# A pool of their own at the top of SBUF for the transposed activations of a two-layer decoder trunk

## The chip, the cores and the metric

The kernel runs on one core of a Trainium2 chip. The metric is the device time of one execution, in microseconds. The kernel before takes 958.66 us (median of three runs, 957.46 to 959.23). The engines are TensorE (PE, with its weight loads as PEld), VectorE (DVE), ScalarE (ACT), GpSimd (POOL) and SyncE (SP), which issues most DMAs.

## What is computed

The reference is a decoder trunk of two layers on 256 tokens of 1024 features, in float32. Layer 0 mixes tokens by differential attention and chunked gated linear attention, layer 1 by a chunked gated DeltaNet. After each mixer come a cross-attention into 256 memory tokens and a gated feed-forward part with a causal convolution of width 3, each followed by a layer norm over `alpha * x + sublayer(x)`.

```python
def memory_cross_attention(x, mem, wq, wkv, wo):
    q = (x @ wq).reshape(B_, S_, N_XA, D_XA)
    k, v = _split(mem @ wkv, (D_MODEL, D_MODEL))
    ...
    return o @ wo

def conv_ffn(x, w_in, conv_w, conv_b, w_out):
    h = causal_dwconv(x @ w_in, conv_w, conv_b)
    g, u = _split(h, (D_FF, D_FF))
    return (jax.nn.silu(g) * u) @ w_out
```

Nearly all of the arithmetic is in such products of 256 tokens with a weight matrix: `D_MODEL` is 1024, `D_FF` is 2816, and a feed-forward input projection has 5632 columns.

## The kernel before

Each float32 product is made of three matmuls on operands split into a high and a low part (`hi` and `lo`, type float32r): high times high, high times low, low times high. A weight piece of 128 x 1024 numbers is loaded by SP into `raw` (pool `rawp`, three buffers of 1 MB), ACT casts it to `wh` (L149) and DVE subtracts to get `wl` (L151); `whp` and `wlp` hold four pieces each. The activations stand transposed in SBUF, features on partitions, as a `Parts` object: four tiles of 128 x 4 x 256, two high and two low, 4096 bytes per partition each. `hT` is the normed input of a sublayer, `uT`, `oT` and `xoT` are the outputs of the mixers and of the cross-attention, `aT` is the feed-forward part's middle (its first four tiles in the same pool, the other eight in a pool of the stage).

There are two forms of projection:

- `mm3` (L156 to L158) has the weights stationary: a 128 x 128 piece of `wh` or `wl` is loaded into the array, and 256 columns of `hT` (or of the transposed memory, `memT`) stream past it. One feature tile of 128 columns takes 8 x 3 = 24 matmuls, and 512 columns take 96. `proj_t_gen` and the loop in `ffn` use it: the results are `ps_t` and `ps_f`.
- `mm3n` (L162 to L164) and `proj_lead` (L298) have the activations stationary, 128 x 128 of them, and 512 columns of `wh` or `wl` stream. `proj_n_gen` (`ps_n`) and `out_proj` (`ps_o`) use it.

The cross-attention takes the same two forms for its scores (`xs`: keys `k` stream past the queries `xq`; in layer 1 the split keys bear the name `wh` too) and its values (`xo`: `pT` streams past `v`).

The feed-forward part calls `proj_first` (512 columns by L298, then transposed, L315), then `proj_t` for 512 more, and then runs 36 feature tiles of 24 matmuls, two weight loads for four tiles. ACT and DVE convolve and gate each result (L1306 to L1317). Elsewhere a chain (a mixer or a cross-attention) is written as a generator, and `weave` puts steps of projections between its steps; TensorE's order is then the order of the code. Each engine works through its own instructions in order, and a semaphore wait holds all that stands behind it.

All pools but the temporary ones are stacked from the bottom of SBUF: constants, `rawp`, `whp`, `wlp`, `tp`, `hp`, `lnp`. The stages' own pools (`pool(...)`, side right) are stacked downwards from the top. `tp` is the pool that the change is about: eight buffers under one tag, handed out in turn to `hT`, `uT`, `xoT`, `oT`, four tiles of `aT`, and three tiles that the DeltaNet holds (`keep`). `new_t` (L383) takes four of them.

Of the kernel before, what the change touches and what calls it, by code (L numbers as in the profile page):

```python
# [74 lines left out]
class Parts:  # L75
    """hi and lo parts of [128, k, 256], four k to a tile"""
# [12 lines left out]
def hybrid_trunk(ctx: ExitStack, tc: tile.TileContext, a: dict, const: dict, out: bass.AP, dbg=None):  # L89
# [6 lines left out]
    tp = ctx.enter_context(tc.tile_pool(name="tp", bufs=8))  # L96
# [5 lines left out]
    def pool(name, bufs=2, side="right"):  # L102
        return tc.tile_pool(name=name, bufs=bufs, side=side, reuse_waits="tile")

# [30 lines left out]
    # ------------------------------------------------------------ weights  # L135
# [6 lines left out]
    normed = []  # last instructions of the layer norms  # L142
# [11 lines left out]
    def mm3(ps, lh, ll, rh, rl, first, last):  # L154
        """weights stationary"""
        nc.tensor.matmul(ps, lh, rh, start=first, stop=False)  # L156
        nc.tensor.matmul(ps, lh, rl, start=False, stop=False)  # L157
        nc.tensor.matmul(ps, ll, rh, start=False, stop=last)  # L158

    def mm3n(ps, lh, ll, rh, rl, first, last):  # L160
        """activations stationary"""
        nc.tensor.matmul(ps, lh, rh, start=first, stop=False)  # L162
        nc.tensor.matmul(ps, lh, rl, start=False, stop=False)  # L163
        nc.tensor.matmul(ps, ll, rh, start=False, stop=last)  # L164
# [5 lines left out]
    def ahead(gen, n):  # L170
        """gen with its items made n steps before they are given"""
        items = []
        for item in gen:
            items.append(item)
            if len(items) > n:
                yield items.pop(0)
        yield from items

    def proj_t_gen(xs, w, c0, n, cb, step=256):
        """cb(m, ps): ps[feature, token] of the columns c0 + 128 m."""  # L180
        def pieces():
            for q in range(0, n, step):
                nq = min(step, n - q)
                raw = load(w, c0 + q, nq)
                for m in range(0, nq, P):
                    nm = min(P, nq - m)
                    yield (q + m) // P, nm, split(raw[:, :, m:m + nm])

        for m, nm, (wh, wl) in ahead(pieces(), AHEAD):
            ps = acc("ps_t")[:nm, :T]  # L190
            for k in range(KT):
                mm3(ps, wh[:, k], wl[:, k], xs.h(k), xs.l(k), k == 0, k == KT - 1)
                if k % 2 and k < KT - 1:
                    yield
            cb(m, ps)
            yield
# [4 lines left out]
    def proj_16(xs, w, c0):  # L201
        """[32, token]: two parts, their sum being the product with 16 columns"""
        raw = load(w, c0, 16)
        hl = whp.tile([P, 1024], F32R, tag="wh", name="w16")[:, :KT * 32].rearrange("p (k i n) -> p k i n", k=KT, i=2)
        nc.scalar.copy(hl[:, :, 0], raw)
        nc.vector.tensor_tensor(hl[:, :, 1], raw, hl[:, :, 0].bitcast(F32), op=ALU.subtract)
        ps = acc("ps_16")[:32, :T]
        for k in range(KT):
            for i, x in enumerate((xs.h(k), xs.l(k))):
                nc.tensor.matmul(ps, hl[:, k].rearrange("p i n -> p (i n)"), x, start=k == i == 0,  # L210
                                 stop=k == KT - 1 and i == 1)
        return ps

    def proj_n_gen(xs, w, c0, n, cb):
        """cb(q, tt, ps): ps[token, feature] of the columns c0 + 512 q."""
# [27 lines left out]
    class Fill:  # L243
        """generators to take steps of, one after the other"""
# [15 lines left out]
    def weave(chain, fill):  # L260
        """the tensor engine's work of the chain, each step of it (n) followed by n steps of fill"""
        with tc.manual_schedule(engines={mybir.EngineType.PE}):
            due = 0.0
            for n in chain:
                due += n
                while due >= 1.0:
                    fill.step()
                    due -= 1.0

    def steps(n, *gens):  # L270
        """the steps of gens in turn"""
        gens = list(gens)
        while gens:
            for gen in list(gens):
                m = next(gen, gens)
                if m is gens:
                    gens.remove(gen)
                else:
                    yield n if m is None else m

    def proj_lead(xs, w, c0, n, cb, step=4, after=()):
        """as proj_n for up to 512 columns, token tile 0 first; after: calls to make after the loads, by number"""
# [19 lines left out]
    def proj_first_gen(xs, w, c0, n, cb):  # L302
        """as proj_t for up to 512 columns, by way of [token, feature], token tile 0 first"""
# [18 lines left out]
    def out_proj(xs, w, nk, order, ntail=NTAIL):  # L322
        """[head, tail]: generators, tail(cb, pools) with generators cb(tt, [half 0, half 1]); the tail has the last 4 of nk"""
# [43 lines left out]
    # ------------------------------------------------- activations, layer norm  # L367
    def to_t_gen(dst, src, tt):
        """token-major src [128, 1024] to the columns of token tile tt of dst"""
# [13 lines left out]
    def new_t(name):  # L383
        return Parts(*[[tp.tile([P, 4, T], F32R, tag="T", name=name) for _ in range(2)] for _ in range(2)])
# [48 lines left out]
    # ------------------------------------------------------------ start  # L433
    # convolution weights, features on partitions
# [31 lines left out]
    def mem_kv0(memT, kp, vp):  # L466
        """hi and lo parts of k [features, memory] and v [memory, features]"""
# [5 lines left out]
    def mem_kv1(memT, kp):  # L473
        """as they are: k0, k1, v0, v1"""
# [14 lines left out]
    def lower(x, lev):  # L489
        """the columns in the lower halves of the blocks of 2 << lev"""  # L490
        return x.rearrange("... (n u j) -> ... n u j", u=2, j=1 << lev)[..., 0, :]

    def upper(x, lev):
        """the columns in the upper halves of the blocks of 2 << lev"""
        return x.rearrange("... (n u j) -> ... n u j", u=2, j=1 << lev)[..., 1, :]

    # ------------------------------------------------------------ layer 0 mixer
    lam_col, conv_w = [], []

    def mixer_ab(h, hT, ap_, fill, res):  # L500
# [7 lines left out]
        # gains of the head norms, features on partitions  # L508
# [4 lines left out]
        def head_out(po, tt, gate, gi, factor, sm):  # L513
            """po [128 t, 4 heads, 128]: rms norm per head, gain (and gate), transposed into uT"""
# [26 lines left out]
        # ---- A projections (token-major, rotary on 16 of 64)  # L541
# [13 lines left out]
        with pool("gla") as sm:  # L555
            # ---- GLA projections
            # rows: the two parts of the low-rank gates' product, the bias
# [58 lines left out]
            def rotary():  # L616
                # rotary tables [128, tt, 8]
# [27 lines left out]
                # lambda on every partition  # L645
# [11 lines left out]
            # ---- GLA  # L657
# [22 lines left out]
            def intra(u):  # L680
                tt, pr = u
                tsl = slice(tt * P, tt * P + P)
                # level l has entries in the columns t of the upper halves of the blocks of 2 << l only
# [49 lines left out]
            def gla():  # L733
                """steps of the tensor engine's work; a step's results are not used in the next one"""
# [43 lines left out]
    def diff_attention(uT, qkv, head_out, sm, nlam):  # L778
        """steps of the tensor engine's work; a step's results are not used in the next one"""
# [82 lines left out]
    # ------------------------------------------------------------ layer 1 mixer  # L862
    def mixer_c(h, hT, sm, smq, fill, res):
# [9 lines left out]
        # per token and head: beta, g and its sums  # L873
# [10 lines left out]
        table = []          # the last to use the table of exp or of silu: the other's users wait  # L884
# [70 lines left out]
        # of group 0, where the next group's are made meanwhile  # L955
# [12 lines left out]
        def col(x):  # L968
            """[P, 4] as [P, 4, 128]"""
            return x.unsqueeze(2).broadcast_to([x.shape[0], 4, P])  # L970
# [25 lines left out]
        def gdn_pre(grp, tt, o):  # L996
# [4 lines left out]
            # decay [s, t] = exp(gc_t - gc_s), t >= s in the chunk  # L1001
# [26 lines left out]
            # with k_n = r k, r^-2 = sum(k^2) + eps: (I + diag(r) G diag(r b)) = diag(r) (I + G diag(r^2 b)) diag(1 / r)  # L1028
            # for G = k k^T decay, so k, v / r and r^2 b take the place of k_n, v and b
            # q_n = q rq, rq = d^-1/2 rsqrt(sum(q^2) + eps); eps / rq^2 is for the norm of the output  # L1030
# [22 lines left out]
            # L[t, s] = k_t.k_s decay b_s below the diagonal; Z^T = (I + L)^-1, by doubling of its diagonal blocks  # L1053
# [4 lines left out]
            # at level l the columns (2 b + u) (1 << l) + r of Z are stored at 64 u + (64 >> l) r + b  # L1058
# [8 lines left out]
        def gdn_inv(o):  # L1067
            Z, L = o["Z"], o["L"]
            for lev in range(1, NLEV + 1):
                # the lower halves' rows and columns packed to 64; at the last level they are the first 64  # L1070
# [41 lines left out]
        def gdn_rec(grp, os_, outs):  # L1112
# [3 lines left out]
            def values(o, pvn):  # L1116
                # diag(b) (I + M diag(b))^-1 = (I + diag(b) M)^-1 diag(b)
# [4 lines left out]
            def norm(tt, pon):  # L1122
# [4 lines left out]
                # (pon * rq) * rsqrt(mean((pon * rq)^2) + eps) = pon * rsqrt(mean(pon^2) + eps / rq^2)  # L1127
# [78 lines left out]
    # ------------------------------------------------------------ cross-attention  # L1206
    def cross(h, hT, kv, l, sm, oT, fill, kvp=None):
        """the first steps, then steps of the tensor engine's work"""
# [87 lines left out]
    # ------------------------------------------------------------ feed-forward  # L1296
# [148 lines left out]
```

## Time and profile before

| what | value |
|---|---|
| median of three runs | 958.66 us |
| profiled execution: span from the first to the last instruction | 956.4 us |
| PE, PEld busy | 936.4 us, 837.1 us |
| DVE, ACT, POOL busy | 690.2 us, 530.0 us, 36.3 us |
| mean DMA traffic | 160 GB/s |

The profile's own execution has a span of 956.4 us; 2.3 us of the median lie outside of it. PE's busy time has to be read with care: a matmul row gives a duration of 283 ns for 256 columns, but the next matmul starts long before that is over, since they are pipelined. What a matmul costs TensorE is read from the timeline instead: the distance from its start to the next one's. A timeline row gives the start in us from the span's start, the duration in us, the engine, the line, the operation with its output and inputs, and how many equal instructions were merged.

### The profile page before, as it was taken

The numbers are of one execution on the slowest core, as the hardware profiler recorded it, in microseconds if no ns is written. First come the engines' busy times: TensorE is split into PE (matmuls) and PEld (weight loads), VectorE is DVE, ScalarE is ACT, GpSimd is POOL, SyncE is SP. The second block draws the span as 40 slices with busy tenths as digits, with TensorE's granted clock in tenths as the row PEclk, the third lists the DMA queues.
The fourth block names the chain that finished last, engine by engine and source line by source line (L and its number), as shares of the span: only waits on it lengthen the run. The fifth ranks groups of instructions, "written<-read, shape, count | busy, mean of one in ns | idle before, by whom it ended". The sixth has DMA issues, their size and how long they took to land. (4 is left out here: it accounts for less than half of the span.)

```text
span 956.4 us, 15842 instructions
## 1 busy us (share of the span) xinstructions
PE 936.4 (98%) x6284; PEld 837.1 (88%) x6284; DVE 690.2 (72%) x1155; ACT 530.0 (55%) x945; POOL 36.3 (4%) x49
## 2 busy tenths in 40 slices
PE   7999999999999999999999999999999999999996
PEld 5877798899888999998889998888789799999885
DVE  5497586776468988884687875654696888888564
ACT  4753476345435766663357875664464386666440
POOL 1000001000000000000010000000200100000000
PEclk9999999999999999999999999998999999999999
DMA  8843336554664555555566441211543546555551
GB/s 252 287 136 124 97 132 201 179 167 159 220 220 130 170 189 191 191 190 176 179 192 181 133 133 45 89 45 45 176 139 127 175 162 214 190 184 178 179 173 45
DMA packets 101715, 152.89 MB, mean 160 GB/s; under 512 B 5225, under 2 KB 73673, under 8 KB 101641
## 3 DMA queue, kind: packets, MB, share of 16 engines
q1 hardware_dynamic: 99576, 145.08, 46.3%
q0 software_dynamic: 2064, 6.80, 2.2%
q8 instruction: 50, 0.82, 0.4%
q14 instruction: 25, 0.20, 0.1%
HBM read 150.81 MB, written 1.05 MB: 159 GB/s over the span
## 5 line engine op out<-in xcount | busy, mean ns | idle before, releaser
L151 DVE TENSOR_TENSOR wl<-raw,wh 128x1024 fp32r<-128x1024 f32 x268 | 325.5, 1223 | 120.7 <-ACT wh L149 119.4
L149 ACT CAST wh<-raw 128x1024 fp32r<-128x1024 f32 x268 | 278.8, 1052 | 239.0 <-PE ps_f L157 71.5
L156 PE MATMUL ps_f<-hT,wh 128*128 128x256 f32 x576 | 163.0, 283 | 0.0
L157 PE MATMUL ps_f<-hT,wh 128*128 128x256 f32 x576 | 163.0, 283 | 0.0
L158 PE MATMUL ps_f<-hT,wl 128*128 128x256 f32 x576 | 163.0, 283 | 0.0
L156 PEld LDWEIGHTS ps_f<-hT,wh 128*128 128x128 f32 x576 | 110.6, 192 | 0.0
L157 PEld LDWEIGHTS ps_f<-hT,wh 128*128 128x128 f32 x576 | 110.6, 192 | 0.0
L158 PEld LDWEIGHTS ps_f<-hT,wl 128*128 128x128 f32 x576 | 110.6, 192 | 0.0
L156 PE MATMUL ps_t<-hT,wh 128*128 128x256 f32 x352 | 103.5, 294 | 0.0
L157 PE MATMUL ps_t<-hT,wh 128*128 128x256 f32 x352 | 99.5, 283 | 0.0
L158 PE MATMUL ps_t<-hT,wl 128*128 128x256 f32 x352 | 99.4, 283 | 0.0
L162 PE MATMUL ps_o<-wh,aT 128*128 128x512 f32 x176 | 69.1, 393 | 0.0
L163 PE MATMUL ps_o<-wl,aT 128*128 128x512 f32 x176 | 68.9, 391 | 0.0
L164 PE MATMUL ps_o<-wh,aT 128*128 128x512 f32 x176 | 68.6, 390 | 0.0
L156 PEld LDWEIGHTS ps_t<-hT,wh 128*128 128x128 f32 x352 | 67.2, 191 | 1.1
L157 PEld LDWEIGHTS ps_t<-hT,wh 128*128 128x128 f32 x352 | 67.3, 191 | 0.1
L158 PEld LDWEIGHTS ps_t<-hT,wl 128*128 128x128 f32 x352 | 67.2, 191 | 0.0
L298 PE MATMUL ps<-wh,hT 128*128 128x512 f32 x192 | 54.8, 404 | 0.0
L298 PEld LDWEIGHTS ps<-wh,hT 128*128 128x128 f32 x192 | 36.4, 193 | 8.3 <-DVE hT L377 0.5
L1306 ACT ACTIVATE fy<-ps_f,fcw 128x256 f32<-128x256 f32 x72 | 40.4, 561 | 0.0
L162 PEld LDWEIGHTS ps_o<-wh,aT 128*128 128x128 f32 x176 | 33.0, 188 | 7.6 <-issue 0.5
L924 DVE SCALAR_TENSOR_TENSOR cv<-ps_t,gcw,cv 128x253 f32<-128x253 f32 (+2 forms) x72 | 33.4, 475 | 8.6 <-ACT cv L921 8.1
(359 smaller groups left out, 1847.7 us busy)
## 6 DMA issues: line engine op xcount, KB each, us to landing
raw<-in_ffn_w_in SPq DMA_DIRECT2D x44, 1024.0 KB, 5.2
raw<-in_w_in SPq DMA_DIRECT2D x26, 1024.0 KB, 5.7
raw<-in_ffn_w_out SPq DMA_DIRECT2D x22, 1024.0 KB, 5.0
raw<-in_xa_wkv SPq DMA_DIRECT2D x16, 1024.0 KB, 5.3
raw<-in_w_mix_out SPq DMA_DIRECT2D x8, 1024.0 KB, 5.1
raw<-in_xa_wq SPq DMA_DIRECT2D x8, 1024.0 KB, 7.1
raw<-in_xa_wo SPq DMA_DIRECT2D x8, 1024.0 KB, 5.3
lngb<-in_ln_g POOLq DMA_DIRECT2D x6, 512.0 KB, 4.8
```

What stands on the lines that cost most here:

```text
L149: nc.scalar.copy(hi, src)
L151: nc.vector.tensor_tensor(lo, src, hi.bitcast(F32), op=ALU.subtract)
L156: nc.tensor.matmul(ps, lh, rh, start=first, stop=False)
L157: nc.tensor.matmul(ps, lh, rl, start=False, stop=False)
L158: nc.tensor.matmul(ps, ll, rh, start=False, stop=last)
L162: nc.tensor.matmul(ps, lh, rh, start=first, stop=False)
L163: nc.tensor.matmul(ps, lh, rl, start=False, stop=False)
L164: nc.tensor.matmul(ps, ll, rh, start=False, stop=last)
L298: nc.tensor.matmul(ps, x, ww[:, k], start=k0 + k == 0 and ww is wh and not xl, stop=k0 + k == KT - 1 and ww is wl)
L924: nc.vector.scalar_tensor_tensor(y[:, d:], ps[:, :T - d], cw[:, j, m:m + 1], y[:, d:], op0=ALU.mult, op1=ALU.add)
L1306: nc.scalar.activation(yt, ps, AF.Identity, scale=cw[:, 2, mc:mc + 1], bias=cw[:, 3, mc:mc + 1])
```

## The change

`tp` has four buffers and not eight. A new pool `xp` of four buffers is opened right after the function `pool`, on the right side and before any stage's pool, so that it lies at the very top of SBUF. `new_t` takes the four tiles of `hT` from `xp`, and those of every other name from `tp`. The diff also strips comments and docstrings, which leaves the lines in place.

```diff
-    tp = ctx.enter_context(tc.tile_pool(name="tp", bufs=8))
+    tp = ctx.enter_context(tc.tile_pool(name="tp", bufs=4))
...
     def pool(name, bufs=2, side="right"):
         return tc.tile_pool(name=name, bufs=bufs, side=side, reuse_waits="tile")
 
+    xp = ctx.enter_context(pool("xp", 4))
+
...
     def new_t(name):
-        return Parts(*[[tp.tile([P, 4, T], F32R, tag="T", name=name) for _ in range(2)] for _ in range(2)])
+        p = xp if name == "hT" else tp
+        return Parts(*[[p.tile([P, 4, T], F32R, tag="T", name=name) for _ in range(2)] for _ in range(2)])
```

The built programs of before and after have the same 9072 instructions in the same order on every engine, and each waits for the same semaphores at the same values. What differs is where the tiles lie. The layout, in bytes from the start of a partition, with the remainder of the address modulo 128, of the tiles that TensorE reads:

| tile | before | mod 128 | after | mod 128 |
|---|---|---|---|---|
| `wh`, `wl` (weight pieces) | 43552 to 76319 | 32 | the same | 32 |
| `hT` | in turn in 76320 to 109087 | 32 | 212960 to 229343 | 96 |
| `uT`, `oT`, `xoT`, first four of `aT` | in turn in 76320 to 109087 | 32 | in turn in 76320 to 92703 | 32 |
| other eight of `aT` | from 188384 | 96 | from 172000 | 96 |
| `memT` | from 162528 | 96 | from 146144 | 96 |
| `k` and `v` of layer 0's cross-attention | from 129760, 146144 | 96 | from 113376, 129760 | 96 |
| `xq` (queries) | from 194464 | 32 | from 178080 | 32 |
| `wh` of `xs` (keys of layer 1) | from 161696 | 32 | from 145312 | 32 |
| `pT` (probabilities) | from 217056 | 96 | from 200672 | 96 |

Inside a tile the pieces that one matmul reads start at multiples of 128 bytes, so the remainder holds for all of them. All pools that stand above `tp`, on both sides, move down by 16384 bytes, which changes no remainder.

## Rows read from the trace of the kernel before

**Rows 1.** The head of the page.

```profile
span 956.4 us, 15842 instructions
```

**Rows 2.** Waits of PE, whole span: total us, times, longest us.

```profile
PE pt L373 <- DMA c_all<-in_const_all: 4.7, 1, 4.7
PE pt L373 <- DMA h<-in_x: 2.4, 1, 2.4
```

**Rows 3.** Instructions that read or write `hT`: durations ns, first and last start.

```profile
L156 PE MATMUL ps_f<-hT,wh x576: 283/283/283, 319.9 to 887.8; 128*128 128x256 f32 x192
...
L156 PE MATMUL ps_t<-hT,wh x352: 277/283/388, 23.3 to 784.1; 128*128 128x256 f32 x176
...
L298 PE MATMUL ps<-wh,hT x192: 387/389/775, 10.7 to 771.2; 128*128 128x512 f32 x192
L298 PE MATMUL ps<-wl,hT x96: 387/389/628, 13.4 to 771.6; 128*128 128x512 f32 x96
L162 PE MATMUL ps_n<-wh,hT x80: 387/397/502, 36.6 to 650.5; 128*128 128x512 f32 x80
```

**Rows 4.** Timeline of PE, feed-forward of layer 0: its first and last rows.

```profile
308.61 0.66 PE L315 MATMUL ps_1t<-c_all,tok 128*128 128x128 f32 x4
...
309.22 0.28 PE L157 MATMUL ps_t<-hT,wh 128*128 128x256 f32 x1
...
423.57 0.40 PE L162 MATMUL ps_o<-wh,aT 128*128 128x512 f32 x1
```

**Rows 5.** Busy us of each engine by stretch: PE, PEld, DVE, ACT, POOL, PEclk, DMA, GB/s.

```profile
309.00:423.50 114.50, 114.50 (x957) 114.50 (x956) 99.91 (x167) 75.35 (x125) 0.00 (x0) 1.00 0.57 187
```

**Rows 6.** Waits of ACT, 309 to 423.5 us: total us, times, longest us.

```profile
ACT wh L149 <- PE ps_f L157: 34.1, 33, 1.1
```

**Rows 7.** Timeline of PE, cross-attention of layer 0 woven with products of `memT`.

```profile
225.66 0.28 PE L156 MATMUL ps_t<-memT,wh 128*128 128x256 f32 x1
...
226.34 0.28 PE L162 MATMUL xs<-k,xq 128*128 128x256 f32 x1
...
230.42 0.28 PE L156 MATMUL xo<-pT,v 128*128 128x256 f32 x1
...
231.74 0.28 PE L158 MATMUL xo<-pT,v 128*128 128x256 f32 x1
...
240.59 0.28 PE L158 MATMUL xo<-pT,v 128*128 128x256 f32 x1
240.71 0.28 PE L156 MATMUL ps_t<-memT,wh 128*128 128x256 f32 x1
...
249.90 0.40 PE L162 MATMUL ps_n<-wh,memT 128*128 128x512 f32 x1
```

**Rows 8.** Timeline of PE, layer 0's attention: a product of `memT` behind transposes.

```profile
137.71 0.60 PE L830 MATMUL pt<-c_all,prob 128*128 128x128 f32 x4
...
138.38 0.28 PE L158 MATMUL ps_t<-memT,wl 128*128 128x256 f32 x1
...
138.95 0.28 PE L157 MATMUL ps_t<-memT,wh 128*128 128x256 f32 x1
```

**Rows 9.** Timeline of PE, cross-attention of layer 1: the scores.

```profile
716.10 0.28 PE L164 MATMUL xs<-wh,xq 128*128 128x256 f32 x1
...
716.46 0.28 PE L164 MATMUL xs<-wh,xq 128*128 128x256 f32 x1
```

**Rows 10.** Timeline of PE, ends of four runs of 512 columns with activations stationary.

```profile
200.36 0.62 PE L298 MATMUL ps<-wl,hT 128*128 128x512 f32 x2
...
202.17 0.28 PE L156 MATMUL ps_t<-hT,wh 128*128 128x256 f32 x1
...
272.30 0.39 PE L162 MATMUL ps_o<-wh,xoT 128*128 128x512 f32 x1
...
445.49 0.39 PE L162 MATMUL ps_o<-wh,aT 128*128 128x512 f32 x1
...
467.69 0.40 PE L163 MATMUL ps_o<-wl,aT 128*128 128x512 f32 x1
```

## The prediction

> **What bounds the kernel now.** I read the waits of PE first, then the timeline of PE in its longest stage, then other stretches of the same instruction form, and last what stands beside PE in that stage. In the whole span of 956.4 us [rows 1] TensorE's two longest waits are 4.7 and 2.4 us [rows 2], both for the first DMAs; nothing later that it waits for is as long. So the time is the sum of what TensorE's instructions cost, and the question is what one costs. That is read from the starts, not from the durations. In the feed-forward part of layer 0 the second of 954 matmuls that follow one another without a break starts at 309.22 us, and the first of the output projection at 423.57 [rows 4]: 40 feature tiles of 24 are 960, six of them stand ahead of the last transposes. So 953 distances take 114.35 us, 120.0 ns each. The granted clock is 1.00 there, the level of 2.4 GHz [rows 5].
>
> Is 120.0 ns what this form costs everywhere? It isn't. In the cross-attention of layer 0, 42 matmuls from 225.66 to 230.42 us (6 on `memT`, 12 scores on `k`, 24 on `memT`) take 4.76 us, 113.3 ns each [rows 7]. The 11 distances from 230.42 to 231.74, `xo` on `pT` and `v`, are again 120.0 ns, and the 78 from 240.71 to 249.90, on `memT`, are 117.8 ns [rows 7]. All of these have 256 moving columns, 128 x 128 stationary numbers, the same types. What goes along with the pace is the place of the two operands in the table of addresses. `hT` with `wh` or `wl` (32 and 32 modulo 128) and `pT` with `v` (96 and 96) have the same remainder: 120.0. `memT` with `wh` (96, 32) and `k` with `xq` (96, 32) are 64 apart: 113.3 or 117.8. The sharpest pair is the scores of the two layers, one piece of code: in layer 0 they run within the 113.3 [rows 7], in layer 1, where `wh` and `xq` both have 32, three distances from 716.10 to 716.46 take 0.36 us, 120.0 ns each [rows 9]. How far apart or how high in SBUF the two lie does not sort them: `pT` and `v` both lie in the upper half and run at 120.0, `k` and `xq` lie there as well and run at 113.3.
>
> **The change, part by part.** Halving `tp` and giving `hT` its own buffers adds no wait: every engine has the same instructions with the same waits at the same values. `oT` now reuses the buffers of the three held tiles, but its writers wait for transposes that stand on PE behind the last matmuls that read those tiles, so this costs nothing, and nothing was hidden by it that could come out. What is left is that `hT` goes from remainder 32 to 96, while all other operands keep theirs. Every pair of `hT` with `wh` or `wl` turns from same to 64 apart, and no other pair changes.
>
> *256 columns of `hT` moving.* There are 576 + 352 in each of three lines [rows 3], 2784 in all. At 113.3 each saves 6.7 ns.
> - The two feed-forward parts: 2 x 953 x 6.7 ns = 12.7 us. Is that stretch bound by PE alone, and will it stay so? ACT waits 33 times for PE to give a weight buffer back, 34.1 us in sum [rows 6]; weight pieces are ready well ahead. DVE is the next to bind: it is busy 99.91 of 114.50 us [rows 5]; in the 108.1 us that would be left it is at 92%, and the loads go from 187 to 198 GB/s. Both fit, so I count the whole gain.
> - `bqk` and the DeltaNet's first k, q and v, four runs of 96 in a row: 384 x 6.7 = 2.6 us.
> - The remaining 2784 - 1920 - 384 = 480 are woven, in runs of 6 to 18 between transposes and small matmuls. Whether so short a run reaches a pace can't be read from the long ones, and the work between may wait for its chain. Between 0 (nothing arrives) and 480 x 6.7 ns = 3.2 us; I take 1.4, somewhat under half.
>
> *512 columns with `hT` stationary.* 192 + 96 in L298 and 3 x 80 in L162 to L164 [rows 3], 528 in all. Here 64 apart seems to cost more, not less. Same remainder: eight matmuls of L298 from 200.36 to 202.17 us take 226.2 ns each [rows 10]. 64 apart: 96 on `memT` from 249.90 [rows 7] to 272.30 take 233.3 ns each; the 97 on the other tiles of `aT` from 445.49 to 467.69 take 228.9 [rows 10], against 228.3 for the 96 on its first tiles ahead of them, 423.57 [rows 4] to 445.49. So between 0.6 and 7.1 ns each, 0.3 to 3.7 us. A gain can't be shut out by one row, but no row shows it. I take 228.9 against L298's 226.2, 2.7 ns, 1.4 us: that on `memT` comes straight behind the 78 at 117.8 [rows 7], and L298's runs have no such run ahead of them.
>
> Sum: 12.7 + 2.6 + 1.4 - 1.4 = **15.3 us less**. The span of 956.4 us [rows 1] would be 941.1; 2.3 us lie outside of it against the median of 958.66, and they stay: **943.4 us**. Its own bounds: with all woven matmuls at full gain and the least loss 12.7 + 2.6 + 3.2 - 0.3 = 18.2, 940.5; with none and the full loss 15.3 - 3.7 = 11.6, 947.1.
>
> **Which of the two paces.** 113.3 and 117.8 ns both occur on the same addresses, so the pace has a memory: the long run at 113.3 goes over from `memT` to `k` and back; after `xo` at 120.0 the next run on `memT` is at 117.8 and stays there [rows 7]. Behind transposes of 128 columns, `memT` runs at 113.3: five distances from 138.38 to 138.95 take 0.57 us [rows 8]. The feed-forward run starts behind transposes too, L315 at 308.61 [rows 4], and has nothing between its 954 matmuls that could throw it over. That is why I take 113.3.
>
> **The rivals.**
> - *The slow one of the two paces.* The run enters at 117.8, as behind `xo`, and holds it to its end, as the 78 do [rows 7]. Then 2784 x 2.2 ns = 6.1 us less 1.4 to 3.7: a time of 954.0 to 956.3, about **955**. For it: nothing shown resets a run. Against it: the transposes ahead of it. If only one of the two feed-forward parts falls into it, 953 x 4.5 ns = 4.3 us of the forecast go: **947.7**.
> - *Addresses don't set the pace.* What I sort by remainder could go with what else those stretches have (woven chains, other buffers), and then nothing changes: **958.7**. For it: I have few kinds of pairs, and no run has `hT` at another remainder. Against it: the scores of the two layers, same code, at 113.3 and 120.0 [rows 7, 9], and `xo` at 120.0 in the middle of runs at 113.3 and 117.8 [rows 7].
> - *Slower.* The 512-column form takes its 7.1 ns on each of 528 matmuls, 3.7 us, while the 256-column form gains nothing because `hT` has something that `memT` has not: **962.4**. The point that decides is a gain of 3.7 us / 2784 = 1.3 ns per 256-column matmul; the smallest seen between a same and a 64-apart pair is 2.2 ns.
>
> The second rival has a rule behind it. The Trainium skill, in "SBUF — State Buffer", section "Who interferes with whom", says that only the port pair of VectorE and GpSimd is contended for, that TensorE's moving reads and weight loads have independent ports, and that PE never waits on anyone; by that rule alone the address of `hT` can't matter and the time would be 958.7. The 120.0 and 113.3 of this trace [rows 7, 9] do not agree with it, and the measurement decides.
>
> **How the numbers follow.** The forecast has a chance of 0.68, one feed-forward part at the slow pace 0.08, both 0.14, no change 0.06, slower 0.04. The predicted time is that of the first, 943.4. Its bounds, 940.5 to 947.1, and the mixed case hold 0.76; to reach 0.8 the range runs into the slow-pace case, so 940 to 955. A measurement of this kernel can tell about 0.2% (1.9 us) from no change: the first three cases are faster by more than that, 0.90; within it 0.06; slower 0.04.
>
> **What the profile after would show.** The first and last row of the feed-forward run: 953 distances of 113.3 ns, 108.0 us, in both layers (117.8 would be 112.3 us, 120.0 again 114.4). ACT still waits there for PE, DVE is busy at about 92%. Runs of L298 at 228 to 233 ns in place of 226. `memT`, `pT` and `xs` at the paces they have now. The prediction is wrong if 256-column runs on `hT` stay at 120.0, if they take 117.8, or if a wait of PE for `wl` from DVE appears in the feed-forward part and takes the gain back.

## The result and the profile after

The changed kernel takes 943.39 us (median of five runs, 941.81 to 943.6), the kernel before beside it 958.12 us (957.46 to 959.23). The ratio is 0.9838, with a 95% interval of 0.9827 to 0.9849. The ratios here and below leave out one disturbed execution, the profiled one of e5_low_192, at 1809 us. The forecast was 943.4 us. That close a hit owes something to errors that cancel, and two of the reasons behind it fell; the later sections show which.

The head of the page after, to be held against [rows 1]: 14.7 us less.

```profile
span 941.7 us, 15842 instructions
```

The feed-forward run of layer 0 on the timeline of PE after, with the rows that answer to [rows 4] (line numbers are two higher than before: L156 is now L158), and then the second and the last row of the same run of layer 1. Columns as there: start in us, duration, engine, line, operation.

```profile
308.11 0.66 PE L317 MATMUL ps_1t<-c_all,tok 128*128 128x128 f32 x4
308.52 0.37 PE L158 MATMUL ps_t<-hT,wh 128*128 128x256 f32 x1
308.73 0.28 PE L159 MATMUL ps_t<-hT,wh 128*128 128x256 f32 x1
...
416.74 0.39 PE L164 MATMUL ps_o<-wh,aT 128*128 128x512 f32 x1
```

```profile
765.49 0.28 PE L159 MATMUL ps_t<-hT,wh 128*128 128x256 f32 x1
...
873.50 0.39 PE L164 MATMUL ps_o<-wh,aT 128*128 128x512 f32 x1
```

953 distances take 416.74 - 308.73 = 108.01 us, and in layer 1 873.50 - 765.49 = 108.01 us: 113.3 ns each, against 120.0 [rows 4]. That is 6.34 us in each layer.

What stands beside TensorE in that stretch, after, with the columns of [rows 5], and the longest wait of ACT there, as [rows 6]:

```profile
308.40:416.80 108.40, 108.40 (x959) 108.40 (x958) 99.85 (x167) 76.93 (x125) 0.00 (x0) 1.00 0.60 197
```

```profile
ACT wh L151 <- PE ps_f L159: 26.4, 32, 0.9
```

DVE is busy 99.85 of 108.40 us, 92%, the loads move 197 GB/s, and ACT still waits 26.4 us for PE to give weight buffers back: the weight pieces are still ready ahead, so the whole gain comes through. The granted clock is 1.00 as before, the level of 2.4 GHz, so the clock has no part in it.

Where the 14.7 us of the span went: I put the matmuls of the two timelines side by side (they have the same order) and added up, per kind, the distance from each start to the next. The six kinds below leave -0.17 us for all other matmuls together.

| kind of matmul | change of the sum, us | forecast, us |
|---|---|---|
| the two feed-forward parts, 256 columns of `hT` | -12.68 | -12.7 |
| `bqk` | -0.61 | } -2.6 |
| first k, q, v of the DeltaNet | -0.75 | } |
| woven runs on `hT` (mixer 1, two cross-attentions) | -1.36 | -1.4 |
| 512 columns with `hT` stationary (L300 and `ps_n`) | +0.63 | +1.4 |
| `memT`, 256 columns | +0.27 | 0 |
| all of it, the rest included | -14.67 | -15.3 |

### The profile page after: what moved, and what is told of

The parts are those of the page before. It is cut to its first block, busy times and chain, and to the rows that moved or that the text cites. A ratio compares the mean times of both kernels' runs of the same rounds, so it can differ in the third digit from the quotient of the medians.

```text
span 941.7 us, 15842 instructions
## 1 busy us (share of the span) xinstructions
PE 921.7 (98%) x6284; PEld 822.2 (87%) x6284; DVE 689.7 (73%) x1155; ACT 533.1 (57%) x945; POOL 36.3 (4%) x49
## 5 line engine op out<-in xcount | busy, mean ns | idle before, releaser
L158 PE MATMUL ps_f<-hT,wh 128*128 128x256 f32 x576 | 159.0, 276 | 0.0
L159 PE MATMUL ps_f<-hT,wh 128*128 128x256 f32 x576 | 159.0, 276 | 0.0
L160 PE MATMUL ps_f<-hT,wl 128*128 128x256 f32 x576 | 159.0, 276 | 0.0
L158 PEld LDWEIGHTS ps_f<-hT,wh 128*128 128x128 f32 x576 | 108.1, 188 | 0.0
L159 PEld LDWEIGHTS ps_f<-hT,wh 128*128 128x128 f32 x576 | 108.1, 188 | 0.0
L160 PEld LDWEIGHTS ps_f<-hT,wl 128*128 128x128 f32 x576 | 108.1, 188 | 0.0
L158 PE MATMUL ps_t<-hT,wh 128*128 128x256 f32 x352 | 102.2, 290 | 0.0
L159 PE MATMUL ps_t<-hT,wh 128*128 128x256 f32 x352 | 98.1, 279 | 0.0
L158 PEld LDWEIGHTS ps_t<-hT,wh 128*128 128x128 f32 x352 | 66.4, 189 | 1.2
L300 PE MATMUL ps<-wh,hT 128*128 128x512 f32 x192 | 55.1, 405 | 0.0
L300 PEld LDWEIGHTS ps<-wh,hT 128*128 128x128 f32 x192 | 36.5, 194 | 8.6 <-DVE hT L379 0.5
L164 PEld LDWEIGHTS ps_o<-wh,aT 128*128 128x128 f32 x176 | 33.0, 188 | 7.6 <-issue 0.5
L166 PEld LDWEIGHTS ps_o<-wh,aT 128*128 128x128 f32 x176 | 33.0, 188 | 7.2
```

Of the source, the lines that this page charges most:

```text
L300: nc.tensor.matmul(ps, x, ww[:, k], start=k0 + k == 0 and ww is wh and not xl, stop=k0 + k == KT - 1 and ww is wl)
```

## The experiments

All of them are about one number: by how many bytes the address of `hT` is ahead of that of a weight tile. Both tiles' addresses are fixed by the layout, so padding moves them. `pad` opens a pool of one tile of n bytes per partition, written once by GpSimd and never read. The "offset" below is address of `hT` minus address of `wh`, modulo 256; before it is 0, after it is 192. The pieces of `hT` and of a weight tile that one matmul reads start at multiples of 512 bytes, so the offset holds for all of them. The FFN pace (FFN: the feed-forward part) of a run is the time from the second matmul of the feed-forward run to the first of `ps_o`, divided by 953, as above. All ratios are against runs of the kernel before on the same chip.

**The first four: a remainder modulo 128?** The prediction had it that an equal remainder modulo 128 gives 120.0 ns and 64 apart gives less. Four layouts, three with `xp` at the top as in the change, one with it low beside `tp`. Their padding adds up to 128 bytes, which shifts the tiles stacked behind it by half of 256 as well; so their times hold more than `hT`'s share, and what is read from them is the FFN pace.

```diff
 # e1_top_same: hT at the top, offset 128
+    pad("pad0", 64)
     xp = ctx.enter_context(pool("xp", 4))
+    pad("pad1", 64)
 # e3_top_32: offset 160                 # e4_top_96: offset 96
+    pad("pad0", 32)                      pad("pad0", 96)
     xp = ...                             xp = ...
+    pad("pad1", 96)                      pad("pad1", 32)
 # e2_low_apart: hT low, offset 64
     tp = ctx.enter_context(tc.tile_pool(name="tp", bufs=4))
+    pad("pad0", 64, "left")
+    xp = ctx.enter_context(tc.tile_pool(name="xp", bufs=4))
+    pad("pad1", 64, "left")
...
-    xp = ctx.enter_context(pool("xp", 4))
```

> The changed kernel with a padding of 64 bytes above the pool of hT and one of 64 bytes below it: hT stays at the top of SBUF in its own pool, but at 212896, remainder 32 modulo 128, the same as that of the weight pieces; every other tile keeps its remainder. If the remainder sets the pace: 256-column matmuls on hT take 120.0 ns again (feed-forward run of 953 distances 114.4 us), L298 226 ns, and the time is that of the kernel before, 958.1 us, within 1 us. If the place at the top of SBUF, far from the weight pieces, or the pool of its own brought the gain: 113.3 ns and 943.4 us, as the changed kernel.

> The pool of hT stands low in SBUF, right above tp, with 64 bytes of padding below it and 64 above: hT at 92768, remainder 96, 64 apart from the weight pieces, in the neighbourhood where it was before the change. If the remainder sets the pace: 113.3 ns (or 117.8) per 256-column matmul on hT, and 943.4 us as the changed kernel if both feed-forward runs take the faster pace, 947.7 if one does, up to 952.5 if none does. If the place at the top is what counts: 120.0 ns and 958.1 us.

> As the first of these, with 32 bytes of padding above the pool of hT and 96 below: hT at the top with remainder 64, 32 apart from the weight pieces. What it tells is how wide the collision is. If only equal remainders modulo 128 cost: 113.3 or 117.8 ns, 943 to 952.5 us. If it is a matter of halves of 128 bytes (32 and 64 lie in different halves, 32 and 0 in the same): also fast here, but slow with 96 apart. If the distance has to be 64 exactly, 120.0 ns and 958 us.

> As the one before, with 96 bytes of padding above and 32 below: hT at the top with remainder 0, 96 apart from the weight pieces. If only equal remainders modulo 128 cost: 113.3 or 117.8 ns, 943 to 952.5 us, as with 32 apart. If what counts is that both lie in the same half of 128 bytes (0 and 32 do): 120.0 ns and 958 us, unlike with 32 apart.

e1_top_same took 957.11 us (ratio 0.9987, 0.9977 to 0.9998), e2_low_apart 954.48 (0.9958, 0.9944 to 0.9973), e3_top_32 955.65 (0.997, 0.996 to 0.998), e4_top_96 959.07 (1.0011, 0.9997 to 1.0024). The timeline of PE of e1_top_same, second row of the feed-forward run of layer 0 and the row that ends it; then the same of e2_low_apart and of e4_top_96:

```profile
309.09 0.28 PE L166 MATMUL ps_t<-hT,wh 128*128 128x256 f32 x1
...
422.18 0.39 PE L171 MATMUL ps_o<-wh,aT 128*128 128x512 f32 x1
```

```profile
312.68 0.28 PE L166 MATMUL ps_t<-hT,wh 128*128 128x256 f32 x1
...
424.92 0.39 PE L171 MATMUL ps_o<-wh,aT 128*128 128x512 f32 x1
```

```profile
309.94 0.28 PE L166 MATMUL ps_t<-hT,wh 128*128 128x256 f32 x1
...
424.30 0.39 PE L171 MATMUL ps_o<-wh,aT 128*128 128x512 f32 x1
```

113.09, 112.24 and 114.36 us for 953 distances: 118.7, 117.8 and 120.0 ns. e1_top_same has the weights' own remainder modulo 128 and should have stood at 120.0; it is 1.3 ns quicker, in a repeating pattern of single distances from 112 to 123 ns. Its time alone, 957.11, lies within the 1 us of 958.1 that the rule allowed; it is the pace that speaks against the rule. e4_top_96, 32 bytes from the weights modulo 128, should have gained and has nothing: its mean is 120.0, though in a pattern from 116 to 125 ns and not flat. e2_low_apart has the 117.8 that was allowed for, but is 2 us over the 952.5 that was named for it. So the rule modulo 128 is wrong. But the pace does move with the padding, so "addresses don't matter" is wrong too. Sorted modulo 256, offset 0 is the flat 120.0 and 128 is something else; and then the pairs of the kernel before sort as well: `pT` with `v`, and `wh` with `xq` in layer 1, have offset 0; `k` with `xq` 64; `memT` with `wh` 192. The weights never move in these kernels, so `hT`'s own remainder changes together with the offset. That it is the difference that counts, the rows before the change support: `pT` has the remainder 224 modulo 256, as `hT` has after, and takes 120.0 ns with `v`, which has 224 too [rows 7]. No run moved the weights.

**The offset modulo 256, and the place.** The next three carry 256 bytes of padding in all, so that no other tile that stands behind it changes its remainder modulo 256.

```diff
 # e5_low_192: hT low, offset 192
     tp = ctx.enter_context(tc.tile_pool(name="tp", bufs=4))
+    pad("pad0", 192, "left")
+    xp = ctx.enter_context(tc.tile_pool(name="xp", bufs=4))
+    pad("pad1", 64, "left")
...
-    xp = ctx.enter_context(pool("xp", 4))
 # e6_top_64: hT at the top, offset 64    # e7_top_0: offset 0
+    pad("pad0", 128)                      pad("pad0", 192)
     xp = ctx.enter_context(pool("xp", 4)) xp = ...
+    pad("pad1", 128)                      pad("pad1", 64)
```

> The four hT buffers lie low in SBUF, beside the shared pool, each 192 bytes further than a weight tile when addresses are counted modulo 256, as in the changed kernel; the other tiles keep their remainders. Theory A (the offset of moving and stationary operand modulo 256 sets the pace, wherever they lie): 256-column matmuls of both FFNs at 113.3 ns as in the changed kernel, FFN 6.3 us shorter each than before, 943.4 us in all. Theory B (a low place is what gave e2_low_apart its 117.8 ns, and the top of SBUF is what gives 113.3): 117.8 ns again, about 954 us. Theory C (offsets 64 and 192 both allow 113.3 and 117.8 and which one comes is set by what stands ahead): either of the two paces in either FFN, 943 to 954.

> The hT buffers lie at the top as in the changed kernel, but 64 bytes further than a weight tile modulo 256, as in e2_low_apart. Theory A (the offset modulo 256 sets the pace): both FFNs at 117.8 ns as in e2_low_apart, 2.1 us shorter each than before, about 953 to 954 us. Theory B (the place at the top gives 113.3): both at 113.3 ns, about 943.4 us. Theory C (64 and 192 are alike, what stands ahead chooses): one of the two paces in either FFN, 943 to 954.

> The hT buffers lie at the top in a pool of their own as in the changed kernel, but at the weights' own remainder modulo 256, as in the kernel before: the pool without the change of remainder. Theory A (the offset modulo 256 sets the pace): a flat 120.0 ns per 256-column matmul in both FFNs as before, 958 us. Theory B (the remainder modulo 128 sets it, as the prediction had it, and e1_top_same left the FFNs at 118.7 for another reason): the FFNs as in e1_top_same, 118.7 ns in a pattern, 957. Theory D (the pool of its own, in place of the shared one, is worth time): well under 957, with hT at 113 to 118 ns.

e5_low_192 took 942.93 us (ratio 0.9839, 0.9824 to 0.9854). No row of its trace is used; e11_low_tails, below, shows the same place and offset. e6_top_64 took 951.93 us (0.9947, 0.9929 to 0.9965), e7_top_0 958.43 us (1.0006, 0.9997 to 1.0015). On the timelines of PE, first of e6_top_64, then of e7_top_0, the feed-forward run of layer 0:

```profile
308.45 0.66 PE L324 MATMUL ps_1t<-c_all,tok 128*128 128x128 f32 x4
308.87 0.37 PE L165 MATMUL ps_t<-hT,wh 128*128 128x256 f32 x1
309.07 0.28 PE L166 MATMUL ps_t<-hT,wh 128*128 128x256 f32 x1
...
421.31 0.40 PE L171 MATMUL ps_o<-wh,aT 128*128 128x512 f32 x1
```

```profile
310.99 0.28 PE L166 MATMUL ps_t<-hT,wh 128*128 128x256 f32 x1
...
425.34 0.40 PE L171 MATMUL ps_o<-wh,aT 128*128 128x512 f32 x1
```

112.24 and 114.35 us: 117.8 and 120.0 ns. e7_top_0 is the whole change (own pool, top of SBUF, `tp` halved) with the remainder put back, and its time is that of before, to 0.15%: pool, place and halving are worth nothing that these times can show, the offset is worth the gain. e5_low_192 is the reverse, the change's offset at a low place, and has the whole gain. And e6_top_64 has the change's place behind the very same four transposes, and the pace of e2_low_apart, 117.8 ns, not 113.3: in the feed-forward runs offset 64 and offset 192 are not alike, although both are "64 apart" modulo 128.

**Between the quarters.**

```diff
 # e9_top_224                             # e10_top_32
+    pad("pad0", 224)                      pad("pad0", 160)
     xp = ctx.enter_context(pool("xp", 4)) xp = ...
+    pad("pad1", 32)                       pad("pad1", 96)
```

> hT at the top, 224 bytes further than a weight tile modulo 256 (the changed kernel: 192). Theory A1 (192 and 64 are two good places, and the pace worsens on either side of them): 118 to 120 ns in the FFNs, 953 to 958 us. Theory A2 (the pace falls steadily from offset 96 to offset 256 less a little, so 224 is at least as good as 192): 113.3 ns or less, down to 106.7 ns for 256 columns at the 2.4 GHz that the granted clock of 0.995 stands for; 6.6 ns less over 1906 distances would be 12.6 us more, 931 to 943.4 us.

> hT at the top, 32 bytes further than a weight tile modulo 256. Theory A1 (64 and 192 are the good places, the pace worsens on either side): 118 to 120 ns in the FFNs, 953 to 958 us. Theory A3 (the pace depends on how far the operands are apart, whichever lies behind, so 32 is as 224 in the other run of this pair): the same pace as there, within 0.5 ns.

e9_top_224 took 956.32 us (0.9985, 0.9972 to 0.9997), e10_top_32 953.08 us (0.9942, 0.9923 to 0.9961). Timelines of PE, e9_top_224 first:

```profile
311.32 0.28 PE L166 MATMUL ps_t<-hT,wh 128*128 128x256 f32 x1
...
424.09 0.39 PE L171 MATMUL ps_o<-wh,aT 128*128 128x512 f32 x1
```

```profile
309.20 0.28 PE L166 MATMUL ps_t<-hT,wh 128*128 128x256 f32 x1
...
420.39 0.39 PE L171 MATMUL ps_o<-wh,aT 128*128 128x512 f32 x1
```

112.77 and 111.19 us: 118.3 and 116.7 ns. Theory A1 named 118 to 120 for both; 224 is in that range, and 32 is quicker than 64, which no theory had. A3 falls with it (118.3 is not 116.7), and A2 as well: in the feed-forward runs 192 is the best of the eight offsets tried, by 3.4 ns. The table of the FFN pace, the same within 0.02 ns in both layers of each profile that is read here:

| offset of `hT`, bytes modulo 256 | ns per matmul | seen in |
|---|---|---|
| 0 | 120.0 | before, e7_top_0 |
| 32 | 116.7 | e10_top_32 |
| 64 | 117.8 | e2_low_apart, e6_top_64 |
| 96 | 120.0 | e4_top_96 |
| 128 | 118.7 | e1_top_same |
| 160 | 118.7 | e3_top_32 |
| 192 | 113.3 | after, e8_tails, e11_low_tails |
| 224 | 118.3 | e9_top_224 |

**The 512-column form, and a better kernel.** For this form the offset 0 is the quick one (226.2 ns on L298 before [rows 10]). In the kernel after, as before the change, two groups of operands lie at other offsets: the weight tiles of the pool `tail`, with which each output projection ends, and the upper tiles of `aT`. 192 bytes of padding bring both to 0. (The first pad stands ahead of the tails of the mixers' and the cross-attentions' output projections, `nk == KT`; the pad ahead of `ff0` and `ff1` shifts `aT` and the feed-forward tails stacked behind it.)

```diff
 # e8_tails: the changed kernel, and
-        with pool("tail", 4) as tailp, pool("gains", 1) as gains:
+        with pool("pad", 1) as padp, pool("tail", 4) as tailp, pool("gains", 1) as gains:
+            if nk == KT:
+                nc.gpsimd.memset(padp.tile([P, 48], F32, name="pad"), 0.0)
...
-    with pool("ff0") as sm:
+    with pool("padf0", 1) as padp, pool("ff0") as sm:
+        nc.gpsimd.memset(padp.tile([P, 48], F32, name="padf"), 0.0)
```

(`ff1` likewise.) e11_low_tails has these lines and the layout of e5_low_192.

> The changed kernel with 192 bytes of padding ahead of the pools of the FFN tails, so that the 512-column pairs of the tails, which now lie 64 or so bytes apart modulo 256, have the same remainder modulo 256. Theory A (the offset modulo 256 sets the pace of 512-column matmuls as well, and for those an equal remainder is the quick case, as 226.7 ns shows where it stood before against 228.9 and 233.3): 4 tails of 47 distances from 233.3 to 226.7 ns, some 194 more from 228.9 to 226.7 ns, 1.7 us in all: about 941.7 us against 943.4. Theory B (512-column matmuls differ by what stands around them, not by address): 943.4 us as the changed kernel, with 233 ns still there.

> hT low in SBUF at offset 192 modulo 256 (as e5_low_192) and the FFN tails at an equal remainder (as e8_tails). Theory A (the offset alone counts, the place does not): 113.3 ns in both FFNs, 227 ns in the tails, 941.8 us as e8_tails, within 1. Theory B (the place at the top has a share in it): FFNs at 117.8 ns, 951 us or more.

e8_tails took 941.79 us (0.9815, 0.9793 to 0.9837), e11_low_tails 941.12 us (0.9819, 0.98 to 0.9838). Timeline of PE, the cross-attention's output projection of layer 0, a stretch of its tail: first after, then e8_tails.

```profile
277.46 0.39 PE L165 MATMUL ps_o<-wl,xoT 128*128 128x512 f32 x1
...
283.29 0.39 PE L166 MATMUL ps_o<-wh,xoT 128*128 128x512 f32 x1
```

```profile
277.46 0.39 PE L165 MATMUL ps_o<-wl,xoT 128*128 128x512 f32 x1
...
283.12 0.39 PE L166 MATMUL ps_o<-wh,xoT 128*128 128x512 f32 x1
```

The same 25 distances take 5.83 us after and 5.66 in e8_tails: 233.2 against 226.4 ns. Added up over the trace, the distances below 300 ns of all output projections (`ps_o`: their tails, and those on `aT`) are some 1.9 us shorter, near the 1.7 expected. The medians differ by 1.6 us, but the intervals of the two ratios overlap and e8_tails' five times run from 938.05 to 942.94 us, so the gain over the change is shown by the rows, and not by the times alone. In e8_tails' own profile a part is given back elsewhere. Two stretches by engine, with the columns of [rows 5], first after, then e8_tails:

```profile
640.00:680.00 40.00, 38.90 (x266) 33.38 (x266) 19.50 (x33) 17.26 (x41) 5.29 (x6) 0.91 0.26 82
```

```profile
640.00:680.00 40.00, 39.44 (x259) 34.26 (x256) 19.68 (x33) 17.05 (x41) 4.27 (x7) 0.87 0.28 92
```

The mean granted clock in these 40 us is 0.87 in place of 0.91: a dip to the lower level, 1.2 GHz, lasts 10.2 us and not 6.8. By the two means that is an estimated 0.04 x 40 = 1.6 us. Such a dip near 650 us stands in every profile that is read here, the one of before too, with lengths from 3.4 to 10.2 us.

In e11_low_tails the feed-forward run of layer 0, on the timeline of PE:

```profile
309.00 0.28 PE L166 MATMUL ps_t<-hT,wh 128*128 128x256 f32 x1
...
417.02 0.39 PE L171 MATMUL ps_o<-wh,aT 128*128 128x512 f32 x1
```

108.02 us, 113.3 ns at the low place: the place has no share in this pace. For the whole time that is not shown: at offset 64 the low e2_low_apart, with its 128 bytes of padding, took 954.48 us and the high e6_top_64 951.93, at one FFN pace.

**One pair of addresses, two paces.** Padding the tails changed something that it did not touch. The run of 96 for the DeltaNet's first k, from its first matmul to its 96th, on the timeline of PE after and then of e8_tails; in both `hT` has offset 192:

```profile
491.85 0.28 PE L158 MATMUL ps_t<-hT,wh 128*128 128x256 f32 x1
...
503.04 0.28 PE L160 MATMUL ps_t<-hT,wl 128*128 128x256 f32 x1
```

```profile
491.18 0.28 PE L158 MATMUL ps_t<-hT,wh 128*128 128x256 f32 x1
...
501.94 0.28 PE L160 MATMUL ps_t<-hT,wl 128*128 128x256 f32 x1
```

95 distances: 11.19 us, 117.8 ns, and 10.76 us, 113.3 ns. The addresses are equal, the instructions ahead of the run are equal, and the paces are the two that the prediction had named. e11_low_tails has 113.3 as well. In e6_top_64 the feed-forward runs stand at 117.8 and this run at 113.3, the other way round; the same 95 distances there:

```profile
496.50 0.28 PE L165 MATMUL ps_t<-hT,wh 128*128 128x256 f32 x1
...
507.27 0.28 PE L167 MATMUL ps_t<-hT,wl 128*128 128x256 f32 x1
```

So offsets 64 and 192 both know both paces. Nor is it these two alone: this run of 96 takes 117.8 ns at offset 32 (FFN 116.7), 117.3 at 160 (118.7) and 120.0 at 224 (118.3). The table above is one of the feed-forward runs, and no law for every run at an offset. What chooses is not found. Remainders alone don't: in e7_top_0 every tile that TensorE reads has its remainder of before, and yet the product of `memT` behind transposes, which ran at 113.3 [rows 8], runs there at 117.6:

```profile
139.99 0.28 PE L166 MATMUL ps_t<-memT,wh 128*128 128x256 f32 x1
...
141.99 0.39 PE L851 MATMUL po_a<-av,aT 128*128 128x128 f32 x2
```

(17 distances, 2.00 us.) Each kernel left one profile, so it is also open whether a run such as this keeps its pace from one execution to the next. The feed-forward runs seem to: all six that were read at offset 192 have 113.3 and all four at 64 have 117.8, and the five times of the changed kernel lie within 1.8 us, while one such run at the other pace would cost 4.3.

## Why the prediction was right, and where it was not

- **TensorE is the bound, and a matmul is costed by the distance of starts.** Right: the span fell by what the distances fell, and no wait of PE came in its place (the two longest are still those for the first DMAs, 4.7 and 2.2 us).
- **The two feed-forward parts, 12.7 us.** Right in size, 12.68, and in its cover: DVE at 92%, 197 GB/s, ACT still waiting for PE.
- **The rule: equal remainder modulo 128 is slow, 64 apart is quick.** Wrong. The period is not 128: offset 128 runs at 118.7 ns (e1_top_same), and offset 96, 32 apart, at 120.0 (e4_top_96). The pairs that I sorted had only the offsets 0, 64 and 192 modulo 256, and with these alone the wrong rule and the better one can't be told apart. The forecast needed the pace at offset 192, and for that `memT` with `wh`, which has it, was the right neighbour, though it ran at both paces. The trace of before held a warning, too: `xo` on `pT` and `v`, counted at 120.0, takes 117.9 and 118.8 ns over twelve distances from 218.19 and from 220.32 us, between products of `hT`.
- **Why 113.3 and not 117.8: "behind transposes".** The reason fell, though the value held, and that is luck. Behind the same four transposes offset 64 gives 117.8 ns (e6_top_64) and offset 192 gives 113.3, in both layers of every profile read at these offsets. The row that I leaned on, `memT` behind transposes at 113.3 [rows 8], has offset 192 as well; but it was no rule for that offset either. Five products of `memT` in layer 0's attention come behind transposes; before the change all five settle at 113.3, after it, with their offset unchanged, four of them run at 117.8, and in e7_top_0 the very run of [rows 8] does. So why the feed-forward runs at offset 192 take the quicker pace stays open; that they do is measured. The rival of the slow pace, at 955, had more to it than its chance of 0.14 said: with 64 bytes of offset in place of 192 it is what happens (951.93 and 954.48).
- **`bqk` and the first k, q, v, 2.6 us.** Too high by 1.2: 0.61 + 0.75 = 1.36. Of the last three runs' matmuls, the runs of 96 and of 143 took 117.8 ns and only one of 49 took 113.7, the entry included. I had given them the pace of the long run without asking which of the two they would enter, although I weighed that question for the feed-forward part.
- **Woven runs, 1.4 us.** 1.36.
- **512 columns with `hT` stationary, +1.4 us.** Right in sign, too high by 0.8: +0.63. The timeline of PE after, the eight matmuls of L300 that answer to those of L298 in [rows 10]:

```profile
199.98 0.62 PE L300 MATMUL ps<-wl,hT 128*128 128x512 f32 x2
...
201.81 0.28 PE L158 MATMUL ps_t<-hT,wh 128*128 128x256 f32 x1
```

  Here they take (201.81 - 199.98) / 8 = 228.8 ns, 2.6 more than before and near the 2.7 that I had taken. But over all 528 the increase is 0.63 us, 1.2 ns each: 0.45 us for the 288 of L300, and 0.18 us for the 240 of `ps_n`, under 1 ns each. The eight rows were the settled end of their run; early in that run ten distances in a row stood at 224 to 236 ns before the change already. So a settled end was priced as if it were the whole.
- **"`memT` at its present pace."** Not quite: its 256-column matmuls cost 0.27 us more in all, with unchanged addresses. More of its runs entered the slower of the two paces, the four named above among them. The prediction had said that the pace has a memory and then left this out of the sum.
- **The other rivals.** "Addresses don't set the pace" is out: e7_top_0 differs from the change by 192 bytes of padding ahead of `xp` and 64 behind it, and is 15.0 us slower (958.43 against 943.39). With it goes what the prediction drew from the rule of the Trainium skill in "SBUF — State Buffer", section "Who interferes with whom", that moving reads and weight loads have independent ports and that PE never waits on anyone: read as saying that the address can't matter, it does not agree with these runs, where eight offsets give paces from 113.3 to 120.0 ns at a granted clock of 1.00. What in the chip makes the difference the runs don't show. "Slower" would need a gain below 1.3 ns per matmul; at offset 96 it was 0, and e4_top_96 is the slowest kernel here, at 959.07, though its interval (0.9997 to 1.0024) still holds no change at all.

So the gain was forecast at 15.3 us and measured at 14.7: the terms that were too good (1.2 on k, q, v and `bqk`, and 0.3 on `memT`) and the one that was too bad (0.8 on the 512-column form) cancel in the main. That the time itself agrees within 0.1 us is luck on top: the prediction started from 958.66 us, and the kernel before measured beside the change took 958.12.

## What to carry to other kernels

Where TensorE never waits and the same form of matmul runs at different distances in different stages, compare the addresses of moving and stationary operands, modulo 256 and not less, before looking for anything in the schedule; an offset of 192 bytes in place of 0 was worth 1.5% here, with not one instruction changed. Take the offset that was measured for the same form in the run that matters (here 192 bytes for the feed-forward runs of 256 columns, 0 for 512 columns), not a rule from two or three pairs, and test it with a pad of 256 bytes split in two, which leaves the remainders of the tiles behind it as they are. Read the pace of every long run afterwards, since one offset can show two. A change of pool is two changes, reuse and address: undo one with padding before crediting the other.

## What the runs showed of the hardware

- In the feed-forward runs a 256-column matmul on split operands shows six paces over eight offsets, from 113.3 to 120.0 ns, at the same granted clock of 1.00; the order over the offsets is not monotonic and not symmetric (32: 116.7, 224: 118.3; 64: 117.8, 192: 113.3). Why is not settled: the runs give the table, not the mechanism.
- The two forms did best at different offsets. At offset 0 the 512-column form takes 226.4 ns and the 256-column form its worst 120.0; at 192 the 256-column form takes its best 113.3, and L300 some 229.
- A pace, once entered, is held: 954 matmuls without a break kept theirs to the last row in every profile, and a run of 96 with equal addresses took 117.8 ns in one kernel and 113.3 in another. Which pace a run enters is not set by the remainders alone (`memT` in e7_top_0), and what sets it is open.
